# A two-layer encoder trunk on one core: attention scores three steps ahead, projection pieces in one run per step

## The chip, the core and the metric

The program runs on one core of one Trainium2 chip. The metric is the time of one execution on the device, in microseconds (us). Before the change it is 2655.66 us, the median of three runs (2654.55 to 2656.12). Beside the times there is one profiled execution with its trace.

## What is computed

Two layers over 2048 frames of 1024 channels. The first is a gated MLP with spatial mixing, the second is a chunked band attention with 16 heads of 64 channels, and it is the second that the change touches. Cut to that:

```python
# K, V come once from the stream after layer A; chunks of 64 frames, band = own chunk and 8 before
def one_chunk(c, qc):
    kc = lax.dynamic_slice_in_dim(k_pad, c * CHUNK, B_BAND, axis=1)
    vc = lax.dynamic_slice_in_dim(v_pad, c * CHUNK, B_BAND, axis=1)
    sc = jnp.einsum('bqhd,bkhd->bhqk', qc, kc) + bias        # clipped relative positions
    sc = jnp.where(valid, sc, NEG_INF)
    return jnp.einsum('bhqk,bkhd->bqhd', jax.nn.softmax(sc, -1), vc)

q, z = jnp.split(h @ w_qz, 2, axis=-1)
x = x + (o * silu(z)) @ w_out            # o: the chunks' results
out = rms_norm(x, final_norm_g)
```

## The kernel before, in words

All products are made of float32 operands that are split in a high and a low part, so each block product is three matmuls: high by high, low by high, high by low (lines L111 to L113, one helper for all of them). Layer A fills the first 1538 us or so; then comes the attention, to the end of the program.

The attention goes through four blocks of 512 frames (`t` = 0 to 3) and in each through eight pairs of heads (`p` = 0 to 7; head `h` is 2p or 2p+1). A pair has eight **steps** `u`: two heads by four blocks of 128 queries. A step consists of

- `score` (L1398): four matmuls (two where t = 0) of 128 queries against 640 keys (128, 256, 384 or 512 where t = 0) into the tile `s`; then on VectorE the sum with the bias and the row minimum in one instruction (`pr`, `nm`, L1406), on ScalarE the exponential with its row sum (L1413), on VectorE the reciprocal (`sl`, L1416), on GpSimd the scaling of the row (L1417);
- `flip` (L1433): up to five transpositions of the scaled tile `pr` into the tile `tp`, which ScalarE copies out (high part of `pt`, L1437) and VectorE subtracts (low part of `pt`, L1438);
- at step 4, and at step 0 of the next pair, `value` (L1458): 16 matmuls (8 where t = 0) of the transposed rows of one whole head with V, into `pv`.

Beside the steps a generator, `ahead(t, p)`, hands out **pieces**: one piece is three matmuls of 128 by 512. Eight pieces make one projection (`pj`): Q of the next pair, then K of the next pair, then the gate Z; in the blocks from t = 1 on some pieces of the output product of the block before (`bo`) follow. Eight pieces end with an eviction on ScalarE and VectorE: Q by L1322 and L1323, K by L1335 and L1336, Z by L1361 and L1362. Each projection's weights are split before it (L228 on ScalarE, L229 on VectorE). The last pair of a block (a border pair) also moves on to the next block's frames.

How many pieces a pair has is `steps_of(t, p)`: 24 in the pairs p = 0 to 6 of t = 0 and p = 0 to 3 of t = 1 (**short pairs** below; in the very first some are taken ahead), 30 to 38 in the others up to p = 6, 24 or 32 in the border pairs of t = 0 to 2 and 25 in the last pair of all. The loop from L1893 on spreads them: after half step number k the generator has been asked for `total * k // per` pieces.

PSUM has eight banks here: four tiles for `pj`, `bo` and `pv` (`pmm`, bufs=4), one tile of two banks for the scores (`bss`, bufs=1, L1284), one tile of two banks for the transpositions (`ptr`, bufs=1, L1277). With one tile each, a score's first matmul can start only when L1406 has read the score before, and a flip's first transposition only when L1438 has read the flip before. The tile `pr` has four buffers.

Each engine takes its instructions in order. A scheduler lays them out from the order of the calls and its own estimates, so an instruction may stand a few places from where the code has it.

Of the kernel before, what the change touches and what calls it, by code (L numbers as in the profile page):

```python
# [22 lines left out]
NT = S // T  # L23
# [3 lines left out]
NPAIR = 8  # L27
# [6 lines left out]
def trunk_kernel(  # L34
# [1244 lines left out]
    with ExitStack() as bctx:  # L1279
# [35 lines left out]
        def project(t, p):  # L1315
            for acc in one(t, p, 1):
                yield
            for hd in range(2):
                qh = sb.tile([P, T], F32R, tag="Q", name=f"Qh{t}_{p}_{hd}", bufs=8)
                ql = sb.tile([P, T], F32R, tag="Q", name=f"Ql{t}_{p}_{hd}", bufs=8)  # L1320
                r, r2 = halves(hd)
                nc.scalar.mul(qh[r, :], acc[r, :], 0.125)  # L1322
                nc.vector.scalar_tensor_tensor(  # L1323
                    ql[r, :], acc[r, :], 0.125, qh[r, :].bitcast(F32),
                    op0=ALU.mult, op1=ALU.subtract,
                )
                for x_ in (qh, ql):
                    nc.sync.dma_start(x_[r2, :].bitcast(F32), x_[r, :].bitcast(F32))
                qt[t, p, hd] = (qh, ql)
            for acc in one(t, p, 0):  # L1330
                yield
            for hd in range(2):
                r, r2 = halves(hd)
                kx = sb.tile([P, 2 * T], F32R, tag="K", name=f"K{t}_{p}_{hd}", bufs=4)
                nc.scalar.copy(kx[r, T:], acc[r, :])  # L1335
                nc.vector.tensor_tensor(  # L1336
                    kx[r2, T:], acc[r, :], kx[r, T:].bitcast(F32), op=ALU.subtract
                )
                if t + 1 < NT:
                    k_store = (khd[t][p][hd], kx[:, T:].bitcast(F32))  # L1340
                    if held:
                        kept.append(k_store)
                    else:
                        nc.sync.dma_start(*k_store)
                if t > 0:
                    nc.sync.dma_start(kx[:, :T].bitcast(F32), khd[t - 1][p][hd])
                kt[t, p, hd] = kx
            if not held:
                keep_all()
# [23 lines left out]
        def load_bias(t, h):  # L1373
            bias = sb.tile([P, 640], F32, tag="bias", name=f"bias{t}_{h}", bufs=2)
            nc.sync.dma_start(
                bias[:],
                reld[h][127 : 127 + P * 767].rearrange("(p c) -> p c", c=767)[:, :640],
            )
            nc.gpsimd.memset(bias[0:64, 576:640], NEG)
            nc.gpsimd.memset(bias[64:128, 0:64], NEG)  # L1380
            bias_t[t, h] = bias

        def score(t, p, u):

            hd, qb = divmod(u, 4)
            h = 2 * p + hd
            if qb == 1 and (h + 1 < NH or t + 1 < NT):
                load_bias(t + (h + 1) // NH, (h + 1) % NH)
            bias = bias_t[t, h]
            kx = kt[t, p, hd]  # L1390
            c0 = 0 if t > 0 else 512 - qb * P
            n = 640 - c0
            koff = qb * P + c0
            ps = pss.tile([P, 2, 512], F32, tag="ss", name=f"s{t}_{h}_{qb}")
            nseg, w = (2, 320) if n == 640 else (1, n)
            for i, q in enumerate(qt[t, p, hd]):
                for sg in range(nseg):
                    mm(  # L1398
                        ps[:, sg, :w], q[:, qb * P : (qb + 1) * P],
                        kx[:, koff + sg * w : koff + (sg + 1) * w],  # L1400
                        start=i == 0, stop=i == 1,
                    )
            pr = sb.tile([P, 640], F32, tag="Pr", name=f"pr{t}_{h}_{qb}", bufs=4)
            nm = sm.tile([P, 1], F32, tag="nm", name=f"nm{t}_{h}_{qb}", bufs=4)
            sl = sm.tile([P, 1], F32, tag="sl", name=f"sl{t}_{h}_{qb}", bufs=4)
            nc.vector.tensor_tensor_reduce(  # L1406
                out=pr[:, c0:].rearrange("p (a b) -> p a b", a=nseg),
                in0=ps[:, :nseg, :w],
                in1=bias[:, c0:].rearrange("p (a b) -> p a b", a=nseg),
                scale=-1.0, scalar=3.0e38, op0=ALU.add, op1=ALU.min,  # L1410
                accum_out=nm[:],
            )
            nc.scalar.activation(  # L1413
                pr[:, c0:], pr[:, c0:], AF.Exp, scale=-1.0, bias=nm[:], accum_out=sl[:]
            )
            nc.vector.reciprocal(sl[:], sl[:])  # L1416
            nc.gpsimd.tensor_scalar(  # L1417
                pr[:, c0:], pr[:, c0:], sl[:], 1.0, op0=ALU.mult, op1=ALU.mult
            )
            prs[t, h, qb] = pr  # L1420
# [405 lines left out]
        def take(gen, n):  # L1826
            for _ in range(n):
                if next(gen, gen) is gen:
                    return

        def run(gen):
            for _ in gen:
                pass
# [16 lines left out]
        def ahead(t, p):  # L1850

            if t > 1 and p == 0:
                next(outs[t - 1])
            if p + 1 < NPAIR:
                yield from project(t, p + 1)
                values(t, p + 1)
                for q in GATES[t][p]:
                    yield from gate(t, q)
                if (t, p) == (1, 4):
                    next(outs[0])  # L1860
                yield from some(outs[t - 1], SHARE[t][p])
            elif t + 1 < NT:
                yield from some(outs[t - 1], SHARE[t][p])
                yield from border(t)
                yield from project(t + 1, 0)
                values(t + 1, 0)
                yield from gate(t + 1, 0)
            else:
                yield from some(outs[t - 1], SHARE[t][p] - 6)
                last_first()  # L1870
                yield from some(outs[t - 1], 6)
                yield from some(outs[t], 13)

        def steps_of(t, p):
            n = 24
            if p + 1 < NPAIR:
                n = 16 + 8 * len(GATES[t][p])
            elif t + 1 == NT:
                n = 13
            return n + SHARE[t][p]  # L1880

        load_bias(0, 0)
        gen = project(0, 0)
        run(gen)
        first = ahead(0, 0)
        for u in range(2):
            take(first, 4)
            score(0, 0, u)
        held.clear()
# [3 lines left out]
        for t in range(NT):  # L1893
            for p in range(NPAIR):
                gen = ahead(t, p) if t + p else first
                total = steps_of(t, p) - (0 if t + p else 8)
                per = 11 if p + 1 == NPAIR and t + 1 < NT else 16
                todo = []
                if t + 1 == NT and p + 1 == NPAIR:
                    o_early[t - 1, 3] = o_right(t - 1)(3)  # L1900
                    todo = last_open()
                if t == 1 and p < 4:
                    todo = o_sums(p, lambda n: half_tile("C", n, 4), lambda n: half_tile(
                        "S", n, 4, F32R
                    ))
                if (t, p) == (0, 3):
                    nc.sync.dma_start(gf[:], fin_g.partition_broadcast(P))
                done = 0
                for u in range(8):
                    if u < 6:  # L1910
                        score(t, p, u + 2)
                    elif p + 1 < NPAIR or t + 1 < NT:
                        score(t + (p + 1) // NPAIR, (p + 1) % NPAIR, u - 6)
                    upto = total * (2 * u + 1) // per
                    take(gen, upto - done)
                    done = max(done, upto)
                    if u == 4:
                        value(t, p, 0)
                    elif u == 0 and before:
                        value(*before, 1)  # L1920
                    flip(t, p, u)
                    drain_all()
                    send_all()
                    square_all()
                    if u and finals:
                        finals.pop(0)()
                    if todo:
                        todo.pop(0)()
                    upto = total * (2 * u + 2) // per
                    take(gen, upto - done)  # L1930
                    done = max(done, upto)
                if t + 1 < NT or p + 1 < NPAIR:
                    run(gen)
                before = t, p
# [61 lines left out]
```

## Time and profile before

| | |
|---|---|
| median of three runs | 2655.66 us |
| span of the profiled execution | 2652.0 us (the page gives no other time for it; 3.7 us below the median) |
| mean granted TensorE clock | 0.996 |
| first score / last matmul of the trace | 1538.1 us / 2642.6 us |
| matmuls in the span | 12960 |

A row of the page's fifth part reads: line, engine, operation, tile written and tiles read, shape, count; then busy time and mean duration in ns; then the engine's idle time just before such instructions and who ended it. A row of the timeline reads: start, duration (for several merged instructions, of all), engine, line, operation, tiles, shape, count, and in brackets the idle time before it with its releaser. In the rows of windows stand, after the stretch, the busy time (and number of instructions) of TensorE's matmuls, its weight loads, VectorE, ScalarE and GpSimd, then the granted clock, DMA share and GB/s. A matmul's duration there is longer than its distance to the next, since matmuls overlap: 128 by 512 shows as 0.39 to 0.40 us and starts every 0.23 us.

### The profile page before, as it was taken

To read this page: it belongs to the slowest core of one execution; us is meant where nothing else is said; L and a number is where in the kernel's file an instruction comes from. 1 tells how busy PE (TensorE), PEld (TensorE's weight loads), DVE (VectorE), ACT (ScalarE), POOL (GpSimd) and SP (SyncE) were. 2 spreads that over 40 slices of the span, in tenths; PEclk is the share of its full clock that TensorE was granted. 3 is DMA by queue.
4 is the path that set the end of the run, shared out by engine and by line. 5 is a ranking of instruction groups with operands and counts; after the bars stand their busy time and mean duration, and the time that the engine had idled before them with its cause. 6 is when DMAs were issued, how large, how long until landed. Compare 5 with 4: busy or idle time off the path is not lost. (4 is left out here: it accounts for less than half of the span.)

```text
span 2652.0 us, 37980 instructions
## 1 busy us (share of the span) xinstructions
PE 2608.0 (98%) x12960; PEld 2181.4 (82%) x12960; DVE 1885.1 (71%) x2944; ACT 1303.2 (49%) x2303; POOL 897.2 (34%) x874
## 2 busy tenths in 40 slices
PE   8999999999999999999989999999999999999997
PEld 7888888888888888888878878888888888888886
DVE  5655676865767667757767767777778777877677
ACT  5422243442533434343356456666666655666564
POOL 3611334142152322203234434344332232332245
PEclk9999999999999999999999999999999999999999
DMA  7898998989989869967776597778787666875667
GB/s 286 313 344 329 346 370 323 323 323 338 330 302 313 308 233 324 331 206 270 280 251 214 186 280 229 231 245 263 252 270 254 226 204 224 255 230 161 195 224 251
DMA packets 273856, 718.72 MB, mean 271 GB/s; under 512 B 28800, under 2 KB 68736, under 8 KB 273664
## 3 DMA queue, kind: packets, MB, share of 16 engines
q1 hardware_dynamic: 273664, 716.31, 78.4%
q8 instruction: 103, 1.69, 0.3%
q14 instruction: 89, 0.73, 0.1%
HBM read 531.12 MB, written 174.59 MB: 266 GB/s over the span
## 5 line engine op out<-in xcount | busy, mean ns | idle before, releaser
L111 PE MATMUL P<-T,S 128*128 128x512 f32 x1248 | 496.2, 398 | 2.1 <-ACT S L434 2.1
L112 PE MATMUL P<-T,S 128*128 128x512 f32 x1248 | 488.2, 391 | 1.1 <-DVE T L437 1.1
L113 PE MATMUL P<-T,S 128*128 128x512 f32 x1248 | 488.6, 391 | 0.0
L1417 POOL TENSOR_SCALAR pr<-pr,sl 128x640 f32<-128x640 f32 (+4 forms) x256 | 209.7, 819 | 530.4 <-DVE sl L1416 445.2
L111 PE MATMUL pj<-hh_b,wh_b 128*128 128x512 f32 x768 | 320.4, 417 | 0.0
L113 PE MATMUL pj<-hh_b,wl_b 128*128 128x512 f32 x768 | 305.0, 397 | 1.2 <-DVE wl_b L229 1.1
L112 PE MATMUL pj<-hl_b,wh_b 128*128 128x512 f32 x768 | 303.4, 395 | 0.1
L1413 ACT ACTIVATE pr<-pr,nm 128x640 f32<-128x640 f32 (+4 forms) x256 | 195.5, 764 | 188.1 <-DVE nm L1406 186.6
L113 PEld LDWEIGHTS P<-T,S 128*128 128x128 f32 x1248 | 234.9, 188 | 50.5
L111 PEld LDWEIGHTS P<-T,S 128*128 128x128 f32 x1248 | 235.5, 189 | 46.9 <-ACT S L434 2.3
L112 PEld LDWEIGHTS P<-T,S 128*128 128x128 f32 x1248 | 235.6, 189 | 46.1 <-DVE T L437 1.3
L1438 DVE TENSOR_TENSOR pt<-tp,pt 128x640 fp32r<-128x640 f32 (+4 forms) x256 | 188.4, 736 | 43.7 <-ACT pt L1437 41.1
L1406 DVE CUSTOM_DVE_ANT_0 pr<-s,bias 128x640 f32<-128x640 f32 (+4 forms) x256 | 187.9, 734 | 35.7 <-PE s L1398 29.8
L1437 ACT CAST pt<-tp 128x640 fp32r<-128x640 f32 (+4 forms) x256 | 159.0, 621 | 54.0 <-PE tp L1433 49.8
L1433 PE MATMUL tp<-ident,pr 128*128 128x128 f32 x1120 | 166.7, 275 | 8.6 <-DVE pt L1438 7.3
L113 PEld LDWEIGHTS pj<-hh_b,wl_b 128*128 128x128 f32 x768 | 144.7, 188 | 36.4 <-DVE wl_b L229 3.8
L1433 PEld LDWEIGHTS tp<-ident,pr 128*128 128x128 f32 x1120 | 130.7, 140 | 43.3 <-issue 13.7
L111 PEld LDWEIGHTS pj<-hh_b,wh_b 128*128 128x128 f32 x768 | 145.8, 190 | 18.1 <-ACT wh_b L228 1.6
L1458 PEld LDWEIGHTS pv<-pt,V 128*128 128x128 f32 x896 | 143.3, 189 | 20.8 <-DVE pt L1438 3.9
L112 PEld LDWEIGHTS pj<-hl_b,wh_b 128*128 128x128 f32 x768 | 145.8, 190 | 17.1 <-DVE hl_b L186 0.6
L1458 PE MATMUL pv<-pt,V 128*128 128x256 f32 (+3 forms) x896 | 154.5, 320 | 2.2 <-ACT pt L1437 1.1
L229 DVE TENSOR_TENSOR wl_b<-raw_b,wh_b 128x1024 fp32r<-128x1024 f32 x96 | 120.4, 1255 | 28.5 <-ACT wh_b L228 27.8
(294 smaller groups left out, 5725.9 us busy)
## 6 DMA issues: line engine op xcount, KB each, us to landing
S<-hsd SPq DMA_DIRECT2D x288, 512.0 KB, 5.3
rw<-in_w_a SPq DMA_DIRECT2D x108, 512.0 KB, 6.3
A<-ytd SPq DMA_DIRECT2D x72, 512.0 KB, 5.7
raw_b<-wk SPq DMA_DIRECT2D x72, 512.0 KB, 4.3
hsd<-S SPq DMA_DIRECT2D x56, 512.0 KB, 4.9
V<-vhd SPq DMA_DIRECT2D x56, 512.0 KB, 5.4
bias<-reld SPq DMA_DIRECT2D x64, 320.0 KB, 4.2
va<-vd SPq DMA_DIRECT2D x32, 512.0 KB, 5.5
```

Of the source, the lines that this page charges most:

```text
L111: first = mm(ps, lh, rh, start=first, stop=False)
L112: mm(ps, lh, rl, start=False, stop=False)
L113: mm(ps, ll, rh, start=False, stop=last)
L229: tv(wl[:], raw[:], wh[:].bitcast(F32), op=sub)
L1406: nc.vector.tensor_tensor_reduce(out=pr[:, c0:].rearrange("p (a b) -> p a b", a=nseg), in0=ps[:, :nseg, :w], in1=bias[:, c0:].rearrange("p ...
L1413: nc.scalar.activation(pr[:, c0:], pr[:, c0:], AF.Exp, scale=-1.0, bias=nm[:], accum_out=sl[:])
L1417: nc.gpsimd.tensor_scalar(pr[:, c0:], pr[:, c0:], sl[:], 1.0, op0=ALU.mult, op1=ALU.mult)
L1433: ins = tpose(tp[:, b, :], pr[:, b * P : (b + 1) * P], ident[:])
L1437: nc.scalar.copy(oh, tp[:, b0:5, :].rearrange("p a b -> p (a b)"))
L1438: nc.vector.tensor_tensor(pt[:, 2560 + o + b0 * P : 2560 + o + 640], tp[:, b0:5, :].rearrange("p a b -> p (a b)"), oh.bitcast(F32), op=ALU ...
L1458: mm(po[:, q0 * P : q1 * P], vtl[t, p][:, i, hs], rhs, start=(i == blocks[0] and j == 0), stop=(i == 7 and j == 1),)
```

## The change

The scores are computed three steps ahead of their flip, not two. The half of a step's pieces that stood between `score` and `value`/`flip` is gone from there, and all pieces of a step follow the flip in one run. In a short pair `per` is 12, so that the 24 pieces are handed out in the steps 0 to 5; in a border pair it is 9 in place of 11, which also ends at step 5. Before the first pair three scores with four pieces each go ahead, not two.

```diff
+        AHEAD = 3
         load_bias(0, 0)
         gen = project(0, 0)
         run(gen)
         first = ahead(0, 0)
-        for u in range(2):
+        for u in range(AHEAD):
             take(first, 4)
             score(0, 0, u)
...
-                total = steps_of(t, p) - (0 if t + p else 8)
-                per = 11 if p + 1 == NPAIR and t + 1 < NT else 16
+                total = steps_of(t, p) - (0 if t + p else 4 * AHEAD)
+                per = 9 if p + 1 == NPAIR and t + 1 < NT else 12 if total <= 24 else 16
...
                 for u in range(8):
-                    if u < 6:
-                        score(t, p, u + 2)
+                    if u + AHEAD < 8:
+                        score(t, p, u + AHEAD)
                     elif p + 1 < NPAIR or t + 1 < NT:
-                        score(t + (p + 1) // NPAIR, (p + 1) % NPAIR, u - 6)
-                    upto = total * (2 * u + 1) // per
-                    take(gen, upto - done)
-                    done = max(done, upto)
+                        score(t + (p + 1) // NPAIR, (p + 1) % NPAIR, u + AHEAD - 8)
                     if u == 4:
                         value(t, p, 0)
                     elif u == 0 and before:
                         value(*before, 1)
                     flip(t, p, u)
```

The order changes most in the last steps of the short pairs. The first place is TensorE in block t = 1, pair p = 1 (heads 2 and 3; `s_4_1` is the score of head 4, query block 1, and `tp_3_3` the flip of head 3, block 3, which is step 7). Before, from the score of step 7 on:

```order
L1398 MATMUL s_4_1_16683<-K_2_0_16618,Qh_2_0_16472 128x320 x2
L1398 MATMUL s_4_1_16683<-K_2_0_16618,Ql_2_0_16473 128x320 x2
L111 MATMUL pj_2_2_16637<-hh_b,wh_b_2_2_16632 128x512
L112 MATMUL pj_2_2_16637<-hl_b,wh_b_2_2_16632 128x512
L113 MATMUL pj_2_2_16637<-hh_b,wl_b_2_2_16633 128x512
L1433 MATMUL tp_3_3_16698<-ident,pr_3_3_16594 128x128 x5
L111 MATMUL pj_2_2_16637<-hh_b,wh_b_2_2_16632 128x512
```

Five more `pj` matmuls follow there before the next score, and six stood ahead of the first row. Now, from the score of step 6 on:

```order
L1398 MATMUL s_4_1_16678<-K_2_0_16604,Qh_2_0_16488 128x320 x2
L1398 MATMUL s_4_1_16678<-K_2_0_16604,Ql_2_0_16489 128x320 x2
L1433 MATMUL tp_3_2_16690<-ident,pr_3_2_16524 128x128 x5
L1398 MATMUL s_4_2_16707<-K_2_0_16604,Qh_2_0_16488 128x320 x2
L1398 MATMUL s_4_2_16707<-K_2_0_16604,Ql_2_0_16489 128x320 x2
L1433 MATMUL tp_3_3_16719<-ident,pr_3_3_16561 128x128 x5
L1398 MATMUL s_4_3_16737<-K_2_0_16604,Qh_2_0_16488 128x320 x2
L1398 MATMUL s_4_3_16737<-K_2_0_16604,Ql_2_0_16489 128x320 x2
L1458 MATMUL pv_3_16749<-pt_3_16585,V_1_16242 128x512
```

The `pj` matmuls have moved ahead of the first row, and score, flip, score, flip, score stand side by side. The second place is VectorE for the same rows: `Z` is the gate whose last piece ends just before the first of these scores, `wl_b` a weight's low half, `so` a sum of output weights that only the first four pairs of t = 1 have. Before:

```order
L1406 ISA pr_4_1_16688,nm_4_1_16689<-s_4_1_16683,bias_4_16494 128x640
L1406 ISA nm_4_1_16689 128x1
L229 TENSOR_TENSOR wl_b_3_1_16739<-raw_b_3_1_16737,wh_b_3_1_16738 128x1024
L1438 TENSOR_TENSOR pt_3_16564<-tp_3_3_16698,pt_3_16564 128x640
L1416 RECIPROCAL sl_4_1_16690<-sl_4_1_16690 128x1
L1362 SCALAR_TENSOR_TENSOR Z_2_16714<-Z_2_16714,pj_2_2_16637 128x512
L1406 ISA pr_4_2_16730,nm_4_2_16731<-s_4_2_16725,bias_4_16494 128x640
L1406 ISA nm_4_2_16731 128x1
```

Now:

```order
L1362 SCALAR_TENSOR_TENSOR Z_2_16704<-Z_2_16704,pj_2_2_16623 128x512
L1406 ISA pr_4_1_16683,nm_4_1_16684<-s_4_1_16678,bias_4_16463 128x640
L1406 ISA nm_4_1_16684 128x1
L371 TENSOR_TENSOR so_4l<-wo_10_16363,so_4h 128x512
L1438 TENSOR_TENSOR pt_3_16585<-tp_3_2_16690,pt_3_16585 128x640
L1416 RECIPROCAL sl_4_1_16685<-sl_4_1_16685 128x1
L1406 ISA pr_4_2_16712,nm_4_2_16713<-s_4_2_16707,bias_4_16463 128x640
L1406 ISA nm_4_2_16713 128x1
L1438 TENSOR_TENSOR pt_3_16585<-tp_3_3_16719,pt_3_16585 128x640
```

The gate's last instruction (L1362) has moved from behind the flips' low parts to ahead of the first score's L1406, and the weight split (L229) has moved out of this stretch. The third place is TensorE in block t = 0, pair p = 1, at the same steps 6 and 7, where scores and flips are narrower. Before:

```order
L112 MATMUL pj_1_2_14140<-hl_b,wh_b_1_2_14133 128x512
L113 MATMUL pj_1_2_14140<-hh_b,wl_b_1_2_14134 128x512
L1398 MATMUL s_4_1_14176<-K_2_0_14122,Qh_2_0_14013 128x256
L1398 MATMUL s_4_1_14176<-K_2_0_14122,Ql_2_0_14014 128x256
L111 MATMUL pj_1_2_14140<-hh_b,wh_b_1_2_14133 128x512
L112 MATMUL pj_1_2_14140<-hl_b,wh_b_1_2_14133 128x512
L113 MATMUL pj_1_2_14140<-hh_b,wl_b_1_2_14134 128x512
L1433 MATMUL tp_3_3_14189<-ident,pr_3_3_14107 128x128 x4
L111 MATMUL pj_1_2_14140<-hh_b,wh_b_1_2_14133 128x512
```

Now:

```order
L1398 MATMUL s_4_1_14179<-K_2_0_14117,Qh_2_0_14027 128x256
L1398 MATMUL s_4_1_14179<-K_2_0_14117,Ql_2_0_14028 128x256
L1433 MATMUL tp_3_2_14189<-ident,pr_3_2_14063 128x128 x3
L1398 MATMUL s_4_2_14198<-K_2_0_14117,Qh_2_0_14027 128x384
L1398 MATMUL s_4_2_14198<-K_2_0_14117,Ql_2_0_14028 128x384
L1433 MATMUL tp_3_3_14208<-ident,pr_3_3_14092 128x128 x4
L1398 MATMUL s_4_3_14215<-K_2_0_14117,Qh_2_0_14027 128x512
L1398 MATMUL s_4_3_14215<-K_2_0_14117,Ql_2_0_14028 128x512
L1458 MATMUL pv_3_14225<-pt_3_14108,V_1_13793 128x512
```

Here too the `pj` matmuls between score and flip, and between flip and score, have gone to the steps before.

## The prediction

> **What bounds the kernel now.** I read the head of the page first, then, for the attention (from 1538 us on), the waits of TensorE, longest first.
>
> ```profile
> span 2652.0 us, 37980 instructions
> PE 2608.0 (98%) x12960; PEld 2181.4 (82%) x12960; DVE 1885.1 (71%) x2944; ACT 1303.2 (49%) x2303; POOL 897.2 (34%) x874
> ...
> PE tp L1433 <- DVE pt L1438: 7.3, 12, 1.1
> PE s L1398 <- DMA Qh<-Qh: 1.4, 1, 1.4
> PE bo L112 <- DVE wbo L1633: 1.3, 2, 0.7
> PE s L1398 <- DVE nm L1406: 1.1, 2, 0.7
> PE pv L1458 <- ACT pt L1437: 1.1, 1, 1.1
> PE pv L1458 <- DVE pt L1438: 1.0, 3, 0.4
> PE tp L1433 <- POOL pr L1417: 0.6, 1, 0.6
> ```
>
> TensorE's matmuls are busy in 98% of the span, and the change removes and adds no matmul; their order alone changes. So the time is the matmuls' own work plus TensorE's waits, and all that better order can take away in the attention stands in these rows: 7.3 for transpositions that find the one `tp` tile not yet read by VectorE, 1.1 for scores that find the one `s` tile unread, 2.1 for products with V whose `pt` is late, 0.6 for a row that GpSimd had not scaled. That is 11.1 us. The other rows (Q's first copy, `wbo` at the very end) the change leaves alone.
>
> Most of what remains has one place, the last pair, where VectorE is the busy engine (35.62 of 38 us) and not the order:
>
> ```profile
> 2572.00:2610.00 38.00, 32.61 (x172) 25.67 (x171) 35.62 (x61) 24.44 (x47) 21.11 (x19) 1.00 0.89 296
> ```
>
> **The change, part by part.** *Longer lead.* A step of a pair with 31 pieces keeps its work: four scores, five transpositions, about twelve `pj` matmuls, every fourth time a product with V. Each tile of PSUM is asked for again one whole step later, before and after, so the two single tiles gain nothing from a longer lead; what gains is `pr`, which now has three steps for its way over four engines. I give it the 0.6 of the GpSimd row, and half of the 7.3 because VectorE's work is a little more evenly spread: 3.6. Bounds: 0 to all 11.1.
>
> The two waits of products with V stand together at one place, where they cost more than the row says:
>
> ```profile
> 1587.43 0.39 PE L113 MATMUL pj<-hh_b,wl_b 128*128 128x512 f32 x1
> 1588.92 0.50 PE L1458 MATMUL pv<-pt,V 128*128 128x512 f32 x1 [1.10 <-ACT pt L1437]
> 1589.87 1.74 PE L1458 MATMUL pv<-pt,V 128*128 128x512 f32 x7 [0.45 <-DVE pt L1438]
> ...
> 1588.00:1592.00 4.00, 2.63 (x10) 2.24 (x11) 3.05 (x7) 2.37 (x7) 1.09 (x3) 0.80 0.93 275
> 1592.00:1596.00 4.00, 4.00 (x16) 3.18 (x15) 2.76 (x6) 0.96 (x4) 1.84 (x1) 0.77 0.68 247
> ```
>
> Right behind 1.55 us of waits the granted clock falls: 0.80 and 0.77 over two stretches of 4 us, so 4 x 0.20 + 4 x 0.23 = 1.7 us of TensorE are lost beside the waits. I let the change remove this place: 2.1 + 1.7. The credit is 0.6 + 3.6 + 3.8 = **8 us** (0 to 12.8).
>
> *Steps without pieces.* `per` = 12 and 9 end the pieces with step 5. In the program order after the change the steps 6 and 7 of seven pairs in t = 0, of four in t = 1 and of three border pairs consist of score, flip, score, flip, score with no `pj` between: 14 places. What hid VectorE's and ScalarE's work there is gone. Before, the nearest place is the border from t = 1 to t = 2, where one flip follows its score at once and five `pj` matmuls cover the rest:
>
> ```profile
> 2029.66 0.46 PE L1398 MATMUL s<-K,Qh 128*128 128x320 f32 x2
> 2029.86 0.60 ACT L1361 ACTIVATE Z<-pj 128x512 f32<-128x512 f32 x1 [0.45 <-PE pj L113]
> 2030.42 0.74 PE L1433 MATMUL tp<-ident,pr 128*128 128x128 f32 x5
> 2030.49 0.69 DVE L1362 SCALAR_TENSOR_TENSOR Z<-Z,pj 128x512 f32<-128x512 f32 x1 [0.22 <-ACT Z L1361]
> 2030.91 0.48 PE L111 MATMUL pj<-hh_b,wh_b 128*128 128x512 f32 x1
> 2031.10 0.82 DVE L1406 CUSTOM_DVE_ANT_0 pr<-s,bias 128x640 f32<-128x640 f32 x1
> 2032.15 0.45 PE L1398 MATMUL s<-K,Qh 128*128 128x320 f32 x2
> 2032.73 0.83 ACT L1413 ACTIVATE pr<-pr,nm 128x640 f32<-128x640 f32 x1
> 2032.73 0.39 PE L1458 MATMUL pv<-pt,V 128*128 128x512 f32 x1
> 2032.88 0.81 DVE L1438 TENSOR_TENSOR pt<-tp,pt 128x640 fp32r<-128x640 f32 x1
> 2033.46 0.19 ACT L1413 ACTIVATION_READ_ACCUMULATOR pr<-pr,nm 128x1 f32 x1
> 2034.28 0.15 DVE L1416 RECIPROCAL sl<-sl 128x1 f32<-128x1 f32 x1
> ...
> 2038.49 0.82 DVE L1438 TENSOR_TENSOR pt<-tp,pt 128x640 fp32r<-128x640 f32 x1
> 2039.46 0.74 PE L1433 MATMUL tp<-ident,pr 128*128 128x128 f32 x5 [0.42 <-DVE pt L1438]
> ```
>
> The order on VectorE there is the one that the change gives the short pairs: Z first, then the score's sum, then the flip. I count from the first score's start. Its L1406 ends at 2031.92, so at 2.26. VectorE's end reaches TensorE 0.15 later (2039.31 to 2039.46): the next score starts at 2.41. TensorE's own work until then is 0.58 for four scores (2032.15 to 2032.73) and 0.49 for five transpositions (2030.42 to 2030.91): it waits 2.41 - 1.07 = 1.34. The low part of the flip (0.82) then ends at 3.00 and frees `tp` at 3.15; TensorE is through with the second score at 2.99 and waits 0.16. The second score's L1406 stands behind the first one's reciprocal, and that behind the exponential: 2.26 + 0.83 + 0.19 + 0.15 = 3.43, + 0.82 + 0.15 = 4.40; TensorE is through with the second flip at 3.64 and waits 0.76. Together 2.26, say 2.2 us at each of the seven places with t = 1 and borders: 15.4 us.
>
> In t = 0 the tiles are narrower:
>
> ```profile
> L1438 DVE TENSOR_TENSOR pt<-tp,pt 128x384 fp32r<-128x384 f32 x16 | 8.8, 547 | 2.3 <-ACT pt L1437 2.3
> L1406 DVE CUSTOM_DVE_ANT_0 pr<-s,bias 128x384 f32<-128x384 f32 x16 | 8.8, 551 | 1.1 <-PE s L1398 1.0
> L1406 DVE CUSTOM_DVE_ANT_0 pr<-s,bias 128x256 f32<-128x256 f32 x16 | 6.6, 411 | 3.5 <-PE s L1398 3.5
> L229 DVE TENSOR_TENSOR wl_b<-raw_b,wh_b 128x1024 fp32r<-128x1024 f32 x25 | 30.6, 1224 | 14.5 <-ACT wh_b L228 14.2
> ```
>
> There the order is sum (0.41, 256 wide), Z (0.69), low part (0.55), reciprocal (0.15), sum (0.55). I take 0.54 from the first score's start to its sum: two matmuls of 256 columns at 0.23 per 512, some 0.16 more until the last is through, 0.15 of signal. The first sum ends at 0.95, the second score starts at 1.10; Z and the low part end at 2.19, the second flip starts at 2.34; reciprocal and second sum end at 2.89, the third score starts at 3.04. TensorE's own work in between is 0.23 + 0.29 + 0.35 + 0.39 = 1.26, by columns from the same rates (flips of three and four at 0.49 / 5 each). It waits 1.8 us at each of seven places: 12.6.
>
> Sum 28 us. Low end: Z is not in the way, and the first wait shrinks by 0.55: 14 x 1.45 = 20. High end: a weight split of 1.22 (L229, above) or a sum of output weights falls into each: 28 + 17 = 45.
>
> *The clock at these places.* At 1587 a wait of 1.55 us, within 2.2 us, went ahead of a lost 1.7; in the stretch 2572 to 2610 TensorE is without work for 5.4 of 38 us, in smaller gaps, at a clock of 1.00. Waits of 1.8 and 2.2 us within 3 to 4.4 us lie near the first, but spread wider; I let every third of the 14 places lose 1.7: **8 us** (0 to 24).
>
> The Trainium skill, "TensorE: Matmul & The Clock Gate", in its part on the HAM clock gate, has the clock halved after an idle window of about 3.4 us, and its practical rule speaks of idle gaps longer than that; by that rule waits of at most 1.4 us in one piece cost no clock, and the sum would be 8 us lower. The row at 1588 disagrees: there the clock fell with less than half of such a window idle.
>
> *The rest* I take at nothing. K of the next pair is now needed about one run of pieces after its last piece; the scheduler puts part of a score and a flip in between, which covers it, and if not, a few tenths in each of some 14 pairs come on top. The first scores ahead cost nothing, as their pieces are only moved.
>
> The sum: 28 + 8 - 8 = **+28 us** on the span, 2652.0 to 2680.0. The median lies 3.7 above the span of its profile, so 2683.7, rounded to 2684.
>
> **The rivals.**
> *A, no clock is lost.* Gaps at the 14 places stay below what trips the clock, as from 2572 to 2610: 28 - 8 = +20, 2676. For it: those 38 us; against it: 1588. 0.20.
> *B, the clock falls everywhere and VectorE is late.* The gate's end, the splits and the first scores meet in each place; the clock falls at all 14: 28 + 24 - 8 = +44, 2700. For it: VectorE is busy 71% on the page, and 94% in the stretch of the last pair. 0.16.
> *C, no change.* L1406 is ready at once and Z behind it, so that a place costs 0.6: 8 - 8 = 0, 2656. Against it: the score's own 0.58, the 0.82 and the 0.15 alone make 1.55, against 1.07 of TensorE's work. 0.09.
> *D, faster.* The mechanism: two steps without pieces let VectorE catch up, later steps never find a tile unread, and the empty steps' waits do not show. All 12.8 go: 2643. It decides from the point where score to score on VectorE takes less than TensorE's 1.07; the row gives 2.41. For it: the waits removed are real. 0.07.
>
> **How the numbers follow.** The forecast, +28 with some places losing clock, has 0.48 (2676 to 2692). A gives 2676, B 2700, C 2656, D 2643. From the ends of the terms, 20 + 0 - 13 = +7 and 45 + 8 - 8 = +45, the range is 2662 to 2704: it leaves out C, D and the top of B, together some 0.2. About 0.2% (5 us) is what a measurement of this kernel can tell from no change. Slower by more than that: the forecast, A and B, 0.84; within it: C, 0.09; faster: D, 0.07.
>
> **What would show it.** In the profile after, the waits of TensorE list `s` behind `nm` (L1406) with some 14 to 25 us, where 1.1 stands now, and they lie in the last steps of short and border pairs; `tp` behind `pt` stays or grows. The granted clock shows windows below 1.00 between 1560 and 1850, at perhaps five places. If `s` behind `nm` stays under 5 us, the steps without pieces are covered by something that I don't see, and the forecast is wrong; if the sum of waits is right and the time is not, the clock term is.

## The result, and the profile after

| | before | after |
|---|---|---|
| median of four runs | 2655.11 us | 2694.68 us |
| range | 2654.27 to 2656.12 | 2692.06 to 2697.33 |
| ratio | | 1.0148, interval 1.0135 to 1.0162 |
| span of the profiled execution | 2652.0 us | 2692.8 us |
| mean granted TensorE clock | 0.996 | 0.993 |

The change makes the kernel 39.6 us slower by the medians and 40.8 by the two spans. The forecast was 2684, its range 2662 to 2704; the time lies in the range, above the band of the forecast itself (2676 to 2692). First the head of the page of after, then the longest waits of TensorE in the attention: what waits, for whom, the sum in us, how often, the longest.

```profile
span 2692.8 us, 37925 instructions
PE 2619.5 (97%) x12960; PEld 2193.4 (81%) x12960; DVE 1888.4 (70%) x2944; ACT 1302.7 (48%) x2303; POOL 905.7 (34%) x874
...
PE s L1398 <- DVE nm L1406: 14.2, 19, 1.9
PE tp L1433 <- DVE pt L1438: 11.6, 20, 2.0
PE tp L1433 <- DVE sl L1416: 6.8, 10, 1.5
```

The matmuls are as many as before (12960). New are scores that wait for the score before (14.2, where 1.1 stood) and flips that wait behind a reciprocal (6.8, where there was no row); flips behind `pt` grew from 7.3 to 11.6. The `sl` row is put down to the last instruction before the wait's end: the low part of the flip before runs just ahead of that reciprocal and ends after its start, as the next view shows. Of the 11.6, 2.5 lie in the steps without pieces and 3.3 in the last pair, behind 2570; the 5.8 in between stand against 3.7 before, and 2.0 of them are one wait at 1947.

To see where the time went I took the distance from each matmul's start to the next and subtracted what the same pair has in an undisturbed stream (0.231 us for 128 by 512, 0.146 for 320 wide, 0.117 for 256, 0.109 per transposition, 0.09 more for the matmul behind a flip). What is left is **lost time**: waits and lost clock together. Its sums by block move by one or two us with where a block is cut and what is taken as undisturbed, so smaller differences are not read. Up to 2570 us it is 32.9 us before. After, 37.6 us of it lie in the 14 stretches without pieces (seven in t = 0: 19.0; the three borders: 6.4; the first four pairs of t = 1: 12.2), and 30.1 in all the rest. The other 6 us of the 40.8 are 2.6 ahead of the first score, 2.1 behind 2570, and 1.3 that this working does not place. The 2.6 need not be the change's: the first score starts between 1537.7 and 1542.3 in the profiles of this document, at 1538.1, 1537.7 and 1540.3 in three kernels that are the same up to there.

One place of t = 0, pair p = 1, from the timeline of after (start, duration, engine, line, operation, tiles, shape, and in brackets the wait before it):

```profile
1589.45 0.28 PE L1398 MATMUL s<-K,Qh 128*128 128x256 f32 x1
1589.68 0.49 PE L1433 MATMUL tp<-ident,pr 128*128 128x128 f32 x3
1589.88 0.42 DVE L1406 CUSTOM_DVE_ANT_0 pr<-s,bias 128x256 f32<-128x256 f32 x1
1590.28 0.69 DVE L1362 SCALAR_TENSOR_TENSOR Z<-Z,pj 128x512 f32<-128x512 f32 x1
1590.37 0.44 PE L1398 MATMUL s<-K,Qh 128*128 128x384 f32 x1 [0.20 <-DVE nm L1406]
1590.88 0.55 DVE L1438 TENSOR_TENSOR pt<-tp,pt 128x384 fp32r<-128x384 f32 x1
1591.35 0.15 DVE L1416 RECIPROCAL sl<-sl 128x1 f32<-128x1 f32 x1
1591.58 0.63 PE L1433 MATMUL tp<-ident,pr 128*128 128x128 f32 x4 [0.59 <-DVE sl L1416]
1592.02 0.50 PE L1398 MATMUL s<-K,Qh 128*128 128x512 f32 x1
1592.24 0.59 ACT L1437 CAST pt<-tp 128x512 fp32r<-128x512 f32 x1 [1.05 <-PE tp L1433]
1592.88 0.50 PE L1458 MATMUL pv<-pt,V 128*128 128x512 f32 x1
1593.22 0.39 PE L111 MATMUL pj<-hh_b,wh_b 128*128 128x512 f32 x1
```

VectorE has the prediction's order: sum, Z, low part, reciprocal. The second score starts 0.92 after the first (forecast 1.10), the second flip at 2.13 (2.34), the third score at 2.57 (3.04). Lost time here: 1.7 us; the forecast was 1.8, and that the two agree so well is in part luck. The forecast had the third score wait 0.31, and it waits under 0.1; in its place the product with V (L1458) waits for ScalarE's copy of the flip, and 0.4 us are lost there, which the forecast did not have. The border from t = 1 to t = 2:

```profile
2061.66 0.45 PE L1398 MATMUL s<-K,Qh 128*128 128x320 f32 x2
2062.49 0.69 DVE L1362 SCALAR_TENSOR_TENSOR Z<-Z,pj 128x512 f32<-128x512 f32 x1 [1.35 <-ACT Z L1361]
2063.10 0.81 DVE L1406 CUSTOM_DVE_ANT_0 pr<-s,bias 128x640 f32<-128x640 f32 x1
2063.84 0.82 DVE L1438 TENSOR_TENSOR pt<-tp,pt 128x640 fp32r<-128x640 f32 x1
2063.98 0.56 PE L1398 MATMUL s<-K,Qh 128*128 128x320 f32 x2 [1.02 <-DVE nm L1406]
2064.80 0.74 PE L1433 MATMUL tp<-ident,pr 128*128 128x128 f32 x5
2065.87 0.56 PE L1398 MATMUL s<-K,Qh 128*128 128x320 f32 x2 [0.33 <-DVE nm L1406]
```

Second score at 2.32 (forecast 2.41), second flip at 3.14 (3.15), third score at 4.21 (4.40). Lost: 2.03; the forecast was 2.2. In four of the seven places of t = 0 a weight split stands in the row as well, and in the four of t = 1 a sum of output weights (L371, 0.69 us) stands ahead of a low part. Pair p = 3 of t = 0:

```profile
1643.06 1.05 ACT L228 CAST wh_b<-raw_b 128x1024 fp32r<-128x1024 f32 x1 [0.90 <-POOL raw_b L213]
1643.94 0.28 PE L1398 MATMUL s<-K,Qh 128*128 128x256 f32 x1
1644.15 1.22 DVE L229 TENSOR_TENSOR wl_b<-raw_b,wh_b 128x1024 fp32r<-128x1024 f32 x1 [1.79 <-ACT wh_b L228]
1645.29 0.42 DVE L1406 CUSTOM_DVE_ANT_0 pr<-s,bias 128x256 f32<-128x256 f32 x1
1645.77 0.44 PE L1398 MATMUL s<-K,Qh 128*128 128x384 f32 x1 [1.10 <-DVE nm L1406]
```

The score at 1643.94 is done some 0.4 us later, but VectorE has begun the split and reads the score only at 1645.29. The four places with a split in the row lose 2.6 to 3.6 us.

The clock: beside one at the very start of the attention in both (from 1539.2 and 1541.3), five windows of 3.41 us at half the clock lie in the attention after (from 1619.8, 1647.1, 1701.7, 1896.2 and 1947.4), one before (from 1590.4). At 1.7 us each those four more are 6.8 us. Two thirds of these windows' time lie behind the places, so in the 30.1.

### The profile page after: what moved, and what is told of

The parts are those of the page before. It is cut to its first block, busy times and chain, and to the rows that moved or that the text cites. A ratio compares the mean times of both kernels' runs of the same rounds, so it can differ in the third digit from the quotient of the medians.

```text
span 2692.8 us, 37925 instructions
## 1 busy us (share of the span) xinstructions
PE 2619.5 (97%) x12960; PEld 2193.4 (81%) x12960; DVE 1888.4 (70%) x2944; ACT 1302.7 (48%) x2303; POOL 905.7 (34%) x874
## 5 line engine op out<-in xcount | busy, mean ns | idle before, releaser
L1406 DVE CUSTOM_DVE_ANT_0 pr<-s,bias 128x640 f32<-128x640 f32 (+4 forms) x256 | 188.4, 736 | 83.1 <-PE s L1398 71.1
L1433 PE MATMUL tp<-ident,pr 128*128 128x128 f32 x1120 | 168.6, 276 | 19.8 <-DVE pt L1438 11.6
L1458 PE MATMUL pv<-pt,V 128*128 128x256 f32 (+3 forms) x896 | 156.6, 323 | 1.1 <-ACT pt L1437 0.7
L1458 PEld LDWEIGHTS pv<-pt,V 128*128 128x128 f32 x896 | 143.0, 190 | 17.1 <-ACT pt L1437 5.4
L229 DVE TENSOR_TENSOR wl_b<-raw_b,wh_b 128x1024 fp32r<-128x1024 f32 x96 | 121.7, 1269 | 33.0 <-ACT wh_b L228 28.4
```

Source lines behind the costliest of these rows:

```text
L229: tv(wl[:], raw[:], wh[:].bitcast(F32), op=sub)
L1406: nc.vector.tensor_tensor_reduce(out=pr[:, c0:].rearrange("p (a b) -> p a b", a=nseg), in0=ps[:, :nseg, :w], in1=bias[:, c0:].rearrange("p ...
L1433: ins = tpose(tp[:, b, :], pr[:, b * P : (b + 1) * P], ident[:])
L1458: mm(po[:, q0 * P : q1 * P], vtl[t, p][:, i, hs], rhs, start=(i == blocks[0] and j == 0), stop=(i == 7 and j == 1),)
```

## Two theories, and the runs

**W:** the cost is the 14 stretches without pieces and the clock lost behind them; three scores ahead and one run per step cost nothing. **R:** one run per step costs in the filled steps too, since score and flip then stand together and their work on VectorE meets. All runs were compared with the kernel before in the same job (2654.97 for the first four, 2655.78 for the next four, 2657.28 for the last four). The first four runs cut the change into its parts.

**Pieces in all steps.** The changed kernel with its pieces spread over all eight steps, as far as a lead of three allows:

```diff
-                per = 9 if p + 1 == NPAIR and t + 1 < NT else 12 if total <= 24 else 16
+                per = 16
+                full = need = 0
+                if p + 1 == NPAIR and t + 1 < NT:
+                    full, need = total + 8, total + 1
+                elif total == 24:
+                    full, need = 24, 17
...
+                    if full:
+                        upto = (need * (u + 1) + 4) // 5 if u < 5 else need + (full - need) * (u - 4) // 3
```

> The changed kernel, but its pieces are spread over all eight steps again: in a short pair 17 of 24 by the end of step 4 (K must be there for step 5) and the rest in steps 5 to 7, and in the same manner in border pairs; lead of three and one run per step stay. Theory W (the cost is the waits of the 14 places where steps 6 and 7 have no pieces, and the clock behind them): 2654 to 2665 us, scores wait for nm under 4 us. Rival R (the cost is score and flip side by side, which hand VectorE both evictions at once in every step): over 2680 us.

Measured: 2679.5 us, ratio 1.009 (1.0071 to 1.011). The stretches are gone (0.7 us of lost time) and no window of halved clock is left in the attention, but the filled steps now lose 49.6 us, 16.7 more than before. So 15 us came back, not 40: W's number is missed by far, R's (over 2680) by half a us. (The profile's own time is 2673.9, the lowest of the four. Its clock record reads 0.949 nearly throughout, though its matmuls of 128 by 512 start 0.23 us apart as in the others; only the halved windows are read from it.)

**One run per step alone.** The changed kernel with a lead of two and the spread of before:

```diff
-        AHEAD = 3
+        AHEAD = 2
...
-                per = 9 if p + 1 == NPAIR and t + 1 < NT else 12 if total <= 24 else 16
+                per = 11 if p + 1 == NPAIR and t + 1 < NT else 16
```

> Of the change only the one run per step: lead of two and the spread of before (16, and 11 in border pairs) stay. W: 2650 to 2662 us, about as before. R: over 2675 us, since score and flip stand side by side in all steps.

Measured: 2677.0 us, ratio 1.0085 (1.0068 to 1.0102). One run alone costs 22 us, in steps that all have pieces. Its waits of flips:

```profile
PE tp L1433 <- DVE pt L1438: 18.1, 17, 2.3
```

The time is in R's range; whether R's reason holds, the split below decides. The lost time is some 7 us above before in t = 0, 9 in t = 1, and 2 in t = 2 and t = 3 together. The same place comes back in each pair of t = 0; this is p = 2:

```profile
1606.54 1.90 POOL L213 TENSOR_TENSOR raw_b<-raw_b,bg 128x1024 f32<-128x1024 f32 x1
1608.22 0.38 PE L1433 MATMUL tp<-ident,pr 128*128 128x128 f32 x2
1608.47 1.05 ACT L228 CAST wh_b<-raw_b 128x1024 fp32r<-128x1024 f32 x1 [1.78 <-POOL raw_b L213]
1609.43 0.37 ACT L1437 CAST pt<-tp 128x256 fp32r<-128x256 f32 x1
1609.56 1.22 DVE L229 TENSOR_TENSOR wl_b<-raw_b,wh_b 128x1024 fp32r<-128x1024 f32 x1 [2.24 <-ACT wh_b L228]
1610.70 0.68 DVE L1406 CUSTOM_DVE_ANT_0 pr<-s,bias 128x512 f32<-128x512 f32 x1
1611.31 0.42 DVE L1438 TENSOR_TENSOR pt<-tp,pt 128x256 fp32r<-128x256 f32 x1
1611.87 0.52 PE L1433 MATMUL tp<-ident,pr 128*128 128x128 f32 x3 [1.23 <-DVE pt L1438]
```

ScalarE and VectorE stand still for 1.78 and 2.24 us, because the weight split is next in their queues and GpSimd has not scaled the weight. Score and flip are done by 1608.6, but ScalarE's copy of the flip starts only at 1609.43 and VectorE's sum of the score at 1610.70, behind the split, and the next flip waits for them.

**The early end alone.** The kernel before, with the two new values of `per` only:

```diff
-                per = 11 if p + 1 == NPAIR and t + 1 < NT else 16
+                per = 9 if p + 1 == NPAIR and t + 1 < NT else 12 if total <= 24 else 16
```

> Of the change only the early end: the kernel before with 12 pieces' parts in short pairs and 9 in border pairs; lead of two and two half runs stay, so steps 6 and 7 are empty. W: 2672 to 2690 us, most of the loss is there without the rest of the change. R: within 5 us of before.

Measured: 2667.2 us, ratio 1.0052 (1.0032 to 1.0073), between the ranges of W and R. It isn't the empty steps alone, though: with half runs the scheduler fills them. TensorE's order in t = 1, p = 1 shows pieces of the next pair (`pj_3_1`) pulled up between flips and scores; the same places in the changed kernel have none:

```
2 MATMUL s_4_0     1 MATMUL pj_3_1    1 MATMUL tp_3_2 x5   4 MATMUL pj_3_1
2 MATMUL s_4_1     6 MATMUL pj_3_1    1 MATMUL tp_3_3 x5   4 MATMUL pj_3_1
2 MATMUL s_4_2     MATMUL pv_3 ...
```

There is no stretch without pieces in it. Its flips wait 13.1 us for the flip before (7.3 before the change) and 5.8 more that are put down to GpSimd; what brings these the runs did not separate. The changed kernel has no such mix of half runs and early end.

**Z behind the next score's sum.** In the short pairs of the changed kernel L1362 is ordered behind the latest L1406 issued, and the generator's last call, which issues it, moves to the end of the pair:

```diff
+            if late:
+                tc.add_manual_dep(zi.ins, sums[-1], ...)
```

> The changed kernel, but in short pairs Z's last instruction on VectorE is ordered behind the sum of the score of step 7, so that it no longer stands ahead of the sum of the score of step 6. If Z ahead of the sum sets the first wait of a place, as the prediction had it, about 0.55 us go at each of 11 places and perhaps a window or two of half clock: 2685 to 2690 us. If the waits are set by the chain of sum and low part alone: 2693 to 2697 us.

Measured: 2700.9 us, ratio 1.0169 (1.0153 to 1.0185): above both readings, a miss. Z out of the way buys nothing in the sum; scores behind `nm` wait 17.8 us in it. By block the seven places of t = 0 lose 2.3 us less than in the changed kernel, where Z was behind the first sum already, and the four of t = 1, where it stood ahead, 5.0 more. What costs there was not separated.

The next four test what the second run showed: the split's place in the queues. In each a split's two instructions are ordered behind the two evictions of the flip before the last one issued:

```diff
-        tv(wl[:], raw[:], wh[:].bitcast(F32), op=sub)
+        lo = tv(wl[:], raw[:], wh[:].bitcast(F32), op=sub)
+        for ins, name in zip((hi, lo), flipped[-2] if len(flipped) >= 2 else ()):
+            tc.add_manual_dep(ins.ins, name, ...)
...
+            flipped.append((ci.ins.name, si.ins.name))
```

In these kernels the lines below the edit have numbers that are 8 to 12 higher: L1441 or L1444 is the flip, L230 to L232 are the split.

**On one run per step with a lead of two:**

> The kernel before with one run of pieces per step (lead of two, the spread of before; that edit alone gave 2677.0), and the weights' split (ScalarE's copy, VectorE's subtraction) ordered behind the two evictions of the flip before the last one issued, so that it seldom stands ahead of a flip's eviction or a score's sum. Theory S (one run per step costs because the split, late itself, stands in VectorE's and ScalarE's queues ahead of a flip that now follows its score at once): the waits of flips for the flip before fall from 18.1 us to under 8, the time to 2660 to 2668. Rival N (the score's own sum, always ahead of the flip's low part, is the cause, whatever else is in the queue): 2674 to 2680. Rival J (the split comes too late for its own pieces): waits of pj for wl_b or wh_b of over 5 us, 2677 or more.

Measured: 2668.1 us, ratio 1.0041 (1.0025 to 1.0056), and flips wait less than a quarter as long:

```profile
PE tp L1441 <- DVE pt L1446: 4.2, 6, 1.1
PE pj L113 <- DVE wl_b L231: 3.2, 10, 0.8
```

In t = 0 the lost time falls from some 7 above before to 0.6 below it, in t = 1 from some 9 to 5. In t = 2 it rises to some 11 to 12 above, with windows of halved clock from 2186.4 and 2312.7 (6.8 us long): pieces that wait for weights, as J said, and for output weights from DRAM. S has its waits of flips and, at the upper end of its range, its time; J has its waits of pieces (2.7 for `wl_b` and 2.4 for `wh_b` in the attention), but not its time.

**The lead of three with half runs** (the changed kernel with the first half of a step's pieces put back ahead of value and flip):

> The changed kernel with the half of a step's pieces put back between score and flip: a lead of three scores and the early end of the pieces in short and border pairs, but no single run. Beside the early end alone (2667.2) it shows the lead alone. The prediction's reading (the lead changes nothing for the two single tiles, gains at most the 0.6 of the GpSimd row): 2664 to 2669. Rival (a longer lead itself costs, what is left of +39.6 after +22 for one run and +12 for the early end, about 5): 2671 to 2675. Rival (the lead helps the filled steps): under 2662.

Measured: 2676.4 us, ratio 1.0073 (1.005 to 1.0096), above what either reading of the lead had. The interval overlaps that of the early end alone, and its profiled span is 4.0 us above that kernel's; the run does not decide what a lead costs there.

**On the kernel before:**

> The kernel before with the weights' split ordered behind the evictions as in the run of the same job with one run per step; nothing else. If the split ahead of flips costs before too (flips waited 7.3 us, 1.1 of products with V for ScalarE's part of pt and the clock of 1.7 behind it), 2645 to 2652. If its early place is right where halves are used, pieces wait for their weights instead: 2656 to 2665.

Measured: 2654.0 us, ratio 0.9996 (0.9986 to 1.0005), between the two readings. Block by block its profile shows more: lost time is 4.8 us lower in t = 0 and 6.7 higher in t = 1.

**On the changed kernel:**

> The changed kernel with the weights' split ordered behind the evictions, nothing else. Theory S: the cost of one run in filled steps goes, that of the empty steps (score behind nm, 14 us, and the clock) stays: 2676 to 2684, with the waits of flips at under 8 us. Rival N: 2690 to 2697. Rival J (pieces wait for weights): over 2694.

Measured: 2695.3 us, ratio 1.0142 (1.0119 to 1.0166). S's time is missed, and the time lies in the ranges of N and J; the waits of flips are S's (7.9, under 8). The filled steps do lose less (20.3 us), but the late split holds back the first pieces behind a place, which is J's reason, so that the 14 stretches grow and lose 49.0. The run also shows what the split costs inside a place. It stands in no row of the seven places of t = 0 any more, and their scores and flips lose 1.6 to 1.7 us each, 11.6 together; in the changed kernel the same instructions lose 1.6 to 3.2, 17.6 together.

The last four narrow both causes down.

**The kernel before, ordered in t = 0 alone:**

> The kernel before with the weights' split ordered behind the flip's evictions in the block t = 0 alone (there the same order in all blocks had 4.8 us less of waits and lost clock than before, in t = 1 6.7 more). Theory S: 2649 to 2652. If the gain in t = 0 was the luck of one profile (half of it is the one clock window at 1590): 2653 to 2656.

Measured: 2653.2 us, ratio 0.9984 (0.9975 to 0.9994). The time alone is in the range for luck, but the kernel before took 2657.3 beside it, and the ratio, some 4 us, is the gain that the blocks had shown (4.8). The window of halved clock behind 1588 is gone in the profile; its span, 2644.8, is 8 us below the median, so its waits are not read as typical. By 0.16% this kernel is faster than the kernel before.

**One run per step, ordered in t = 0 and t = 1:**

> One run of pieces per step, lead of two, with the split ordered behind the flip's evictions in t = 0 and t = 1 alone (in all four blocks it gave 2668.1, and in t = 2 pieces then waited for their weights, with three windows of halved clock, 11 us more than before). Theory S (one run costs through the split's place and nothing else): 2657 to 2663. Rival N (one run costs by score and flip standing together): over 2666.

Measured: 2664.9 us, ratio 1.0028 (1.0016 to 1.0039), a little above S's range and below N's. The place shown above, with the order:

```profile
1605.91 1.05 ACT L231 CAST wh_b<-raw_b 128x1024 fp32r<-128x1024 f32 x1
1605.97 1.90 POOL L213 TENSOR_TENSOR raw_b<-raw_b,bg 128x1024 f32<-128x1024 f32 x1
1607.00 1.95 DVE L232 TENSOR_TENSOR wl_b<-raw_b,wh_b 128x1024 fp32r<-128x1024 f32 x1 [0.36 <-ACT wh_b L231]
1607.57 0.38 PE L1444 MATMUL tp<-ident,pr 128*128 128x128 f32 x2
1607.98 0.37 ACT L1448 CAST pt<-tp 128x256 fp32r<-128x256 f32 x1 [1.02 <-PE tp L1444]
1609.49 0.41 DVE L1449 TENSOR_TENSOR pt<-tp,pt 128x256 fp32r<-128x256 f32 x1
1610.04 0.30 PE L1444 MATMUL tp<-ident,pr 128*128 128x128 f32 x1
```

The split that is next is one whose weight is there already; the weight that GpSimd is scaling is split later. The next flip starts without a wait. Lost time in t = 0 is 0.8 below before; some 5 stay in t = 1, in part at pieces that wait for `wl_b` (1.6 us in five rows there).

**Both causes taken from the changed kernel** (pieces in all steps, and the order in t = 0 and t = 1):

> The changed kernel with both causes taken away: pieces in all eight steps as in the first run, and the split ordered behind the flip's evictions in t = 0 and t = 1. If the early end of the pieces and the split's place are the whole cost of the change: 2656 to 2664. If the lead of three scores costs by itself: 2666 to 2674. If neither edit reaches the cause: 2678 or more.

Measured: 2677.1 us, ratio 1.0076 (1.006 to 1.0092): in none of the three ranges, so a miss in sum, and clear in its halves. In t = 0 the lost time goes from 5 to 7 above before (pieces in all steps alone) to 1.4 below it. In t = 1 it rises from some 10 to 17.6, at one place in each of the first four pairs:

```profile
1804.05 0.62 ACT L381 CAST so_6h<-wo 128x512 fp32r<-128x512 f32 x1 [2.77 <-DMA ows<-so_5h]
1804.70 0.58 ACT L1346 CAST K<-pj 64x512 fp32r<-64x512 f32 x1
1804.71 0.69 DVE L382 TENSOR_TENSOR so_6l<-wo,so_6h 128x512 fp32r<-128x512 f32 x1 [2.53 <-ACT so_6h L381]
1805.30 0.69 ACT L1448 CAST pt<-tp 128x640 fp32r<-128x640 f32 x1
1806.16 0.82 DVE L1417 CUSTOM_DVE_ANT_0 pr<-s,bias 128x640 f32<-128x640 f32 x1
1807.05 0.56 PE L1409 MATMUL s<-K,Qh 128*128 128x320 f32 x2 [1.80 <-DVE nm L1417]
```

The same mechanism with another culprit: a sum of output weights waits 2.77 us on ScalarE for a store of the sum before it, and K, the flip's copy and the score's sum queue behind. Ordering these sums too was not tried.

**The changed kernel with a lead of two** (`AHEAD = 2`, nothing else):

> The changed kernel with a lead of two scores, nothing else: one run and the early end together. If the two costs only add (22 and 12): 2687 to 2690, and the lead and the halved clock make the rest of 2694.7. If the two together make the longer empty stretch and its halved clock, whatever the lead: 2692 to 2697. If the lead of three is what costs: under 2686.

Measured: 2694.2 us, ratio 1.0142 (1.0128 to 1.0156), the time of the changed kernel (2694.7), and in the range given for "whatever the lead". Again 14 stretches (41.9 us of lost time), while the rest is down to 23.4. Its waits:

```profile
PE s L1398 <- DVE nm L1406: 12.9, 17, 1.2
PE tp L1433 <- DVE sl L1416: 12.4, 11, 2.4
```

With 6.0 behind `pt` its flips wait 18.4 us, as many as in the changed kernel (11.6 and 6.8). So beside one run and the early end the lead of three makes no difference to the time; those two together make all of it.

The lost time up to 2570 us, in us:

| | time | in stretches without pieces | in the rest |
|---|---|---|---|
| before | 2655 | 0 | 32.9 |
| early end, half runs | 2667.2 | 0 | 42.6 |
| one run, three pieces a step | 2677.0 | 0 | 50.2 |
| the same, split ordered in t = 0, 1 | 2664.9 | 0 | 38.4 |
| changed, pieces in all steps | 2679.5 | 0.7 | 49.6 |
| changed, split ordered | 2695.3 | 49.0 | 20.3 |
| changed, lead of two | 2694.2 | 41.9 | 23.4 |
| changed | 2694.7 | 37.6 | 30.1 |

W's place is right for the changed kernel: its loss lies in the 14 stretches. Its numbers failed, because taking the stretches away brought another cost in. R is right that one run costs, but of another kernel and not mainly for its reason: with the split ordered and score and flip still side by side, 8 of its 22 us are left against the kernel before in the same job. With 24 pieces over eight steps, a run of three pieces is shorter than the way of a split through the queues. In the changed kernel the filled steps of the short pairs have four pieces, and there the single run costs nothing. That the fourth piece is what covers the split is argued from this table, not tried alone.

## Why the prediction was right, and where its sizes were off

- **Steps without pieces, 14 places, 28 us.** The places are the ones it named, the order on VectorE too; scores behind `nm` wait 14.2 us, 13.3 of it in the places, at the low end of the 14 to 25 that were to show it. Where only Z and the score's work meet the lost time has the size it gave: 2.03 for 2.2 at the borders with the waits that it named, 1.7 for 1.8 in t = 0 with one wait too many and one too few. The sum is the term that was sized too small: 37.6, with some of the lost clock in it. The prediction put "a weight split of 1.22 (L229, above) or a sum of output weights" at the high end, and eight of the 14 places have one: t = 0 loses 19.0 in place of 12.6, the four pairs of t = 1 12.2 in place of 8.8, the borders 6.4 for 6.6. For t = 0 the split is shown as the cause by the run that orders it out of the places (11.6 for 17.6 in scores and flips); for the sums of output weights in t = 1 no run takes them away.
- **The clock, 8 us.** Five windows of 1.7 us, 8.5. Four of them begin in a place, three of them between 1560 and 1850, where five had been said. The fifth is at a flip of a pair with pieces, so that the size of this term is in part luck. Rival A (no clock lost, 2676) is refuted by these windows, rival B (all 14 lose) too, although the time is nearer to B's 2700 than to 2684: what came on top are the splits, not the clock.
- **The credit, 8 us.** The place at 1588 lost its wait and its clock window, as said. The half of the flips' 7.3 us that more even work on VectorE was to bring did not come. Half of the 7.3, and the 1.1 of scores, lay in the last pair (behind 2570), which the prediction itself had set apart; the rest rose from 3.7 to 5.8. What the filled steps lose still fell, by 2.8 us although it holds 3.8 us more of lost clock, and for a reason that the prediction did not have. Outside the stretches and the halved windows, waits of over 0.15 us went up, from 13.4 to 16.7 us; all smaller excess went down, from 12.6 to 3.0. In good part that is the stream of pieces: from 1545 to 2570 its matmuls start 0.2293 us after one another, where before it was 0.2312. All profiles of kernels with one run have 0.2292 to 0.2298, all with half runs 0.2310 to 0.2314; why, no run shows. So the size of the credit is luck.
- **The longer lead.** "The two single tiles gain nothing from a longer lead" is shown for one run with the early end by the run with a lead of two; with half runs it stays open.
- **The rest at nothing.** One run per step was taken as free. In the changed kernel it is; by itself it costs 22 us, which the prediction did not see, and a change that kept pieces in all steps would have been forecast wrong for that reason.
- **The sum.** 28 was said, 40.8 came: 37.6 in the places (about 3 of it lost clock, where 28 had been said without clock), less 2.8 in the rest, and then 2.1 behind 2570, 2.6 ahead of the first score and 1.3 unplaced, 6.0 that the sum had no term for. The top of the range, 2704, does not follow from the ends given for it: 2652.0 + 45 + 3.7 is 2700.7, which would have held the time too.

## What to carry to other kernels

Where two engines hand a single buffer to and fro, look for what stands between them in the matrix engine's order: pieces of other work are what hides the hand-over, and the price of a stretch without them can be worked out beforehand from the durations of the other engine's row. In an in-order queue the place of side work counts more than its length: with one run per step, a split of 1.2 us that waits for its own input ahead of the critical eviction cost more than the same split ordered behind it, in the blocks where its weights were not needed sooner; in the kernel before, the same order in all blocks gained nothing. Cutting a change into its parts can mislead when a scheduler fills the gaps: the parts alone cost 22 and 12 us, the 22 for a reason that the whole change does not have, the 12 in a kernel without a single empty stretch.

## What the hardware showed

The clock falls in windows on a fixed raster of 3.41 us (all edges of one profile lie a whole number of windows apart), and no window has to be idle throughout for it. The rows give the stretch, TensorE's busy time and, after the five engines, the granted clock; a window with long waits, the one after it, and another such pair:

```profile
1643.70:1647.11 3.41, 1.77 (x11) 1.18 (x10) 2.96 (x7) 2.06 (x5) 0.09 (x1) 0.99 0.42 165
1647.11:1650.52 3.41, 3.41 (x11) 2.48 (x10) 1.71 (x7) 2.01 (x5) 0.97 (x2) 0.51 0.53 154
1824.62:1828.03 3.41, 2.21 (x13) 1.71 (x13) 2.50 (x7) 1.91 (x4) 0.80 (x1) 1.00 0.88 310
1828.03:1831.44 3.41, 3.41 (x21) 2.94 (x19) 2.94 (x6) 2.69 (x6) 1.46 (x1) 1.00 0.87 277
```

Here 1.64 us without a matmul are followed by a halved window and 1.20 are not. It is not a sharp threshold. Over the 14 profiles of this document, from 1545 to 2600, all nine windows with 2.0 us or more without a matmul (up to 2.57) were followed by a halved one. Of the 26 with 1.5 to 2.0 us, 13 were and 13 were not. Below 1.5 us it was two (1.48 and 1.12), and three that continue a window already halved. Waits of 1.8 and 2.2 us per place, which can also fall into two windows, lie where the clock falls about every second time; in the changed kernel it fell at four of the 14. The Trainium skill, "TensorE: Matmul & The Clock Gate", in its part on the HAM clock gate, has a free-running window of 3413 ns, which the raster agrees with, and a practical rule of gaps longer than that, which these rows do not agree with.

VectorE's split of 1.22 us took 1.95 where GpSimd was scaling a weight (the row at 1607.00 above; GpSimd ends at 1607.87, the split 1.08 later). In the profiles of before, after, one run alone and the two kernels with a lead of two and the split ordered, no split of the attention took over 1.4 us without GpSimd at work beside it. The Trainium skill, "SBUF — State Buffer", in the section on two separate sides, has the two engines lock a shared pair of ports in turn where VectorE reads two inputs from SBUF, as the split does; the row agrees.
